# The low part of every weight split, subtracted on VectorE in place of GpSimd

## The chip, the cores and the metric

The kernel runs on one core of a Trainium2 chip. Its engines are TensorE (PE in the profile; PEld is its weight load), VectorE (DVE), ScalarE (ACT), GpSimd (POOL) and SyncE (SP, which issues the DMAs here). Each engine runs its own list of instructions in order and waits for the others through semaphores. The metric is the time on the device in microseconds (us), lower is better.

## The reference

One inference step of a two-layer decoder for 1024 new tokens of one sequence, 8 x 8 tokens of eight running sequences and 16 meta tokens, 1104 columns in all, model width 1024, everything in fp32:

```python
# layer 0
h = h + mamba_mixer(h, ...)        # RMSNorm, in_proj 1024 -> 6176, conv, SSD scan, gated norm, out_proj 2048 -> 1024
h = sq_relu_mlp(h, ...)            # h + square(relu(rmsnorm(h) @ w_up)) @ w_down, 1024 -> 4096 -> 1024
# between
k, v = shared_kv(h, ...)           # one K/V projection
# layer 1
h = h + swa(queries(h), k, v) @ w_o   # sliding window of 128, sinks
h = sq_relu_mlp(h, ...)
y = rmsnorm(h, ...)                # and the conv, SSM and K/V states
```

Nearly all of the arithmetic is in the products with the weights `w_in`, `w_out`, `w_up`, `w_down`, `w_kv`, `w_q`, `w_o`.

## The kernel before

**Split products.** TensorE takes operands rounded to fp32r. To keep fp32 precision each operand is written as a high part, rounded to fp32r, and a low part, the rest. `mm3` (L204 to L206) makes a product from three matmuls: high x high, high x low, low x high. So every weight has to be cast (high) and subtracted (low) on the chip before TensorE can use it; activations are split in the same way elsewhere (for instance at L1230 and L1146 for the inputs of the down product, L1012 for the up product).

**The two weight helpers.** `wunit` loads 128 x 1024 fp32 of a weight into a `raw` tile (two buffers), multiplies it by a norm weight on GpSimd for some (L168), casts it on ScalarE (L170), and subtracts (L171). With `keep` it writes both parts to DRAM, from where they come back later without a split. `wparts` does the same for a quarter block that is already in SBUF, 128 x 512 in the up product and 128 x 384 in the down and out products: cast on ScalarE (L1047), subtract (L1048). The results of both helpers lie in tiles `w`, of which there are six (for four of the units of the out projection's last block there are four more). A cast has to wait until TensorE has released a tile.

**Products of blocks.** The up products (`up_pair`), most of the down products and most of the out projection (`block_products`) compute a 2 x 2 block product with seven products in place of eight. `up_weights` and `down_weights` are generators that yield the seven weights of one output tile: four blocks as they are and three sums, which VectorE makes (L1057 and L1063, L1166 and L1172). The sum `s1` is changed in place at L1063 and L1172 after it was split, so that this step has to follow the subtraction at L1048. One product is 24 or 18 matmuls on two column halves into one of four PSUM tiles (`ma`, `mb`, `mc`, `md`, two banks each), which several of the seven products accumulate in turn. VectorE or ScalarE reads a PSUM tile after a product (L1077 in the up product, L1264 in the down product) before TensorE may go on in it. In the down product the seven inputs of the next block are loaded and split (L1230) while the last products of the block before and the first of the new one run: `make` gives the steps. L1146 splits the inputs of the plain block at the end.

**Stages, in order of time.** The mixer with convolution and SSD scan (to about 600 us), the gates with the grouped norm (to about 870; L763 to L817, with the sum of squares split at L248 and reduced on TensorE at L259 and L262), the out projection (to about 1030), the up product of layer 0 (to about 1460), its down product (to about 1750), K/V and attention (to about 2200), and the up and down products of layer 1 with the final norm. Weights of the attention are split ahead by `split_ahead` in earlier stages.

**What sets the order.** The instructions of an engine are not run in the order of the source: a planner simulates the kernel with its own estimates of every instruction's cost, and each engine gets its list in the order in which that simulation issues them. On the chip the list is fixed. Products and tile counts come from the source.

Of the kernel before, what the change touches and what calls it, by code (L numbers as in the profile page):

```python
# [8 lines left out]
F32 = mybir.dt.float32  # L9
F32R = mybir.dt.float32r  # L10
AF = mybir.ActivationFunctionType
ALU = mybir.AluOpType
# [129 lines left out]
class Kernel:  # L142
# [13 lines left out]
    def wunit(self, view, a, b, pre=None, to=None, key=None, keep=False):  # L156


        nc = self.nc
        if key in self.split:  # L160
            ws = [self.wtile([P, a, b]) for _ in range(2)]
            for e, w in enumerate(ws):
                nc.sync.dma_start(out=w.bitcast(F32), in_=self.split[key][:, e].rearrange("p (a b) -> p a b", b=b))
            return ws
        raw = self.raw([P, a, b])
        nc.sync.dma_start(out=raw, in_=view)
        if pre is not None:
            nc.gpsimd.tensor_tensor(out=raw, in0=raw, in1=pre, op=ALU.mult)  # L168
        wh, wl = ((to or self.wtile)([P, a, b]) for _ in range(2))
        nc.scalar.copy(out=wh, in_=raw)  # L170
        nc.gpsimd.tensor_tensor(out=wl, in0=raw, in1=wh.bitcast(F32), op=ALU.subtract)  # L171
        if keep:
            d = self.split[key] = self.dram.tile([P, 2, 1024], F32, name="ws_%s" % "_".join(map(str, key)))
            for e, w in enumerate((wh, wl)):
                nc.sync.dma_start(out=d[:, e].rearrange("p (a b) -> p a b", b=b), in_=w.bitcast(F32))
        return wh, wl
# [867 lines left out]
    def wparts(self, src, shape):  # L1044
        nc = self.nc
        t = self.wtile([P, 2] + shape)
        nc.scalar.copy(out=t[:, 0], in_=src)  # L1047
        nc.gpsimd.tensor_tensor(out=t[:, 1], in0=src, in1=t[:, 0].bitcast(F32), op=ALU.subtract)  # L1048
        return t[:, 0], t[:, 1]

    def up_weights(self, layer, f):
# [975 lines left out]
```

## Time and profile before

| | |
|---|---|
| three runs | 2921.8, 2928.17, 2928.39 us; median 2928.17 |
| span of the profiled execution | 2921.9 us, beside a lowest run of 2921.8 |
| mean granted clock of TensorE in it | 0.986 |
| GpSimd, the two subtractions (L171, L1048) | 96 and 476 instructions |
| GpSimd idle until ScalarE's casts ended (L170, L1047) | 189.3 and 609.6 us |
| bytes moved | 433 MB, 148 GB/s read and written over the span |

How to read it: a row of a group gives the line, the engine, the operation, output <- inputs, the shapes, the count, then busy us and mean ns of one, then the idle time of the engine before these instructions and what ended it. A row of the waits gives the engine and the line that waited, whom it waited for, and us in total, times, and the longest. Idle time of an engine that nothing waits for costs nothing, and a busy TensorE is not a TensorE at its peak, as the ends of its pipelined matmuls are modelled.

### The profile page before, as it was taken

To read this page: it belongs to the slowest core of one execution; us is meant where nothing else is said; L and a number is where in the kernel's file an instruction comes from. 1 tells how busy PE (TensorE), PEld (TensorE's weight loads), DVE (VectorE), ACT (ScalarE), POOL (GpSimd) and SP (SyncE) were. 2 spreads that over 40 slices of the span, in tenths; PEclk is the share of its full clock that TensorE was granted. 3 is DMA by queue.
4 is the path that set the end of the run, shared out by engine and by line. 5 is a ranking of instruction groups with operands and counts; after the bars stand their busy time and mean duration, and the time that the engine had idled before them with its cause. 6 is when DMAs were issued, how large, how long until landed. Compare 5 with 4: busy or idle time off the path is not lost.

```text
span 2921.9 us, 51729 instructions
## 1 busy us (share of the span) xinstructions
PE 2816.2 (96%) x19895; PEld 2711.0 (93%) x19895; DVE 1895.0 (65%) x2995; ACT 1413.9 (48%) x2742; POOL 1386.1 (47%) x1279
## 2 busy tenths in 40 slices
PE   8999999988989999999999999999999999999998
PEld 6999999978889999999999999988889999999998
DVE  6788777765657675455466765666678454356675
ACT  6555555544555264444343325655555444433333
POOL 5566666665546615444266573312112444345562
PEclk9999999999999999999999999999999999999998
DMA  3344544447655224444554422447453444533422
GB/s 137 91 128 124 125 128 123 123 123 258 218 206 171 80 85 149 136 156 139 224 212 171 161 89 94 160 153 261 164 187 133 150 140 150 206 138 124 151 96 73
DMA packets 219470, 433.43 MB, mean 148 GB/s; under 512 B 30728, under 2 KB 128392, under 8 KB 216648
## 3 DMA queue, kind: packets, MB, share of 16 engines
q1 hardware_dynamic: 219224, 430.14, 44.3%
q8 instruction: 156, 2.56, 0.4%
q14 instruction: 90, 0.74, 0.1%
HBM read 302.71 MB, written 128.32 MB: 148 GB/s over the span
## 4 chain that ended last, share of the span: by engine, by line
PE 77%; DVE 10%; ACT 4%; issue 3%; DMA 3%; POOL 3%; SPq 0%; DVEq 0%; ACTq 0%; POOLq 0%
PE g L204 10%; PE g L206 10%; PE g L205 10%; PE mc L204 4%; PE mc L206 3%; PE mc L205 3%; PE ma L204 3%; PE ma L205 3%; PE ma L206 3%; PE md L206 3%; PE md L205 3%; PE md L204 3%; PE mb L206 3%; PE mb L204 3%; PE mb L205 3%
## 5 line engine op out<-in xcount | busy, mean ns | idle before, releaser
L1048 POOL TENSOR_TENSOR w<-s,w 128x384 fp32r<-128x384 f32 (+1 forms) x272 | 370.4, 1368 | 386.9 <-ACT w L1047 354.4
L206 PE MATMUL g<-S,w 128*128 128x384 f32 (+2 forms) x1584 | 531.1, 336 | 3.9 <-POOL w L171 3.3
L204 PE MATMUL g<-S,w 128*128 128x384 f32 (+2 forms) x1584 | 533.4, 337 | 1.3 <-DVE qp L1462 0.6
L205 PE MATMUL g<-S,w 128*128 128x384 f32 (+2 forms) x1584 | 533.6, 337 | 0.0
L1048 POOL TENSOR_TENSOR w<-raw,w 128x384 fp32r<-128x384 f32 (+1 forms) x204 | 264.3, 1301 | 286.2 <-ACT w L1047 255.2
L171 POOL TENSOR_TENSOR w<-raw,w 128x1024 fp32r<-128x1024 f32 x96 | 247.1, 2574 | 253.3 <-ACT w L170 189.3
L206 PEld LDWEIGHTS g<-S,w 128*128 128x128 f32 x1584 | 301.9, 191 | 5.8 <-POOL w L171 3.6
L204 PEld LDWEIGHTS g<-S,w 128*128 128x128 f32 x1584 | 301.3, 190 | 4.7 <-issue 1.5
L205 PEld LDWEIGHTS g<-S,w 128*128 128x128 f32 x1584 | 301.7, 190 | 0.9 <-issue 0.3
L1047 ACT CAST w<-s 128x384 fp32r<-128x384 f32 (+1 forms) x272 | 149.8, 557 | 313.0 <-DVE s L1172 84.7
L204 PE MATMUL ma<-S,w 128*128 128x276 f32 (+1 forms) x808 | 235.2, 291 | 8.0 <-DVE us L1264 6.7
L206 PE MATMUL ma<-S,w 128*128 128x276 f32 (+1 forms) x808 | 234.7, 290 | 0.0
L205 PE MATMUL ma<-S,w 128*128 128x276 f32 (+1 forms) x808 | 234.3, 290 | 0.0
L1047 ACT CAST w<-raw 128x384 fp32r<-128x384 f32 (+1 forms) x204 | 111.8, 555 | 154.6 <-PE mc L206 45.2
L602 DVE SCALAR_TENSOR_TENSOR fm<-xp,cv,fm 128x1024 f32<-128x1024 f32 x96 | 162.8, 1698 | 33.1 <-ACT fm L583 32.5
L204 PEld LDWEIGHTS ma<-S,w 128*128 128x128 f32 x808 | 153.3, 190 | 9.3 <-ACT S L1229 2.7
L205 PE MATMUL g<-R,w 128*128 128x384 f32 (+2 forms) x480 | 158.6, 330 | 0.0
L204 PE MATMUL g<-R,w 128*128 128x384 f32 (+2 forms) x480 | 158.1, 329 | 0.0
L206 PE MATMUL g<-R,w 128*128 128x384 f32 (+2 forms) x480 | 158.1, 329 | 0.0
L205 PEld LDWEIGHTS ma<-S,w 128*128 128x128 f32 x808 | 153.5, 190 | 0.0
L206 PEld LDWEIGHTS ma<-S,w 128*128 128x128 f32 x808 | 153.2, 190 | 0.0
L170 ACT CAST w<-raw 128x1024 fp32r<-128x1024 f32 x96 | 100.5, 1047 | 105.8 <-DMA raw<-in_w_o_dram 19.9
(492 smaller groups left out, 8696.0 us busy)
## 6 DMA issues: line engine op xcount, KB each, us to landing
raw<-in_w_up_dram SPq DMA_DIRECT2D x64, 512.0 KB
raw<-in_w_in_dram SPq DMA_DIRECT2D x48, 512.0 KB
raw<-in_w_downs_dram SPq DMA_DIRECT2D x64, 384.0 KB
w<-ws_o SPq DMA_DIRECT2D x48, 512.0 KB
w<-ws_q SPq DMA_DIRECT2D x40, 512.0 KB
ab<-acs_d SPq DMA_DIRECT2D x64, 256.0 KB
S<-t_d SPq DMA_DIRECT2D x18, 828.0 KB
S<-t_e SPq DMA_DIRECT2D x18, 816.0 KB
```

The source lines that it names most:

```text
L170: nc.scalar.copy(out=wh, in_=raw)
L171: nc.gpsimd.tensor_tensor(out=wl, in0=raw, in1=wh.bitcast(F32), op=ALU.subtract)
L204: mm(out=out, lhsT=wh, rhs=xh, start=(first and k == 0), stop=False)
L205: mm(out=out, lhsT=wh, rhs=xl, start=False, stop=False)
L206: mm(out=out, lhsT=wl, rhs=xh, start=False, stop=(k == n - 1))
L602: nc.vector.scalar_tensor_tensor(out=acc[:, :SEQ], in0=xp[:, k:k + SEQ], scalar=cv[:, j, k:k + 1], in1=acc[:, :SEQ], op0=ALU.mult, op1=ALU ...
L1047: nc.scalar.copy(out=t[:, 0], in_=src)
L1048: nc.gpsimd.tensor_tensor(out=t[:, 1], in0=src, in1=t[:, 0].bitcast(F32), op=ALU.subtract)
```

## The change

The engine of the subtraction is another in both helpers. Nothing else in the source is changed: the operands, the tiles and their counts stay.

```diff
@@ wunit
         nc.scalar.copy(out=wh, in_=raw)
-        nc.gpsimd.tensor_tensor(out=wl, in0=raw, in1=wh.bitcast(F32), op=ALU.subtract)
+        nc.vector.tensor_tensor(out=wl, in0=raw, in1=wh.bitcast(F32), op=ALU.subtract)
@@ wparts
         nc.scalar.copy(out=t[:, 0], in_=src)
-        nc.gpsimd.tensor_tensor(out=t[:, 1], in0=src, in1=t[:, 0].bitcast(F32), op=ALU.subtract)
+        nc.vector.tensor_tensor(out=t[:, 1], in0=src, in1=t[:, 0].bitcast(F32), op=ALU.subtract)
```

On GpSimd remain the products and copies of the SSD scan and the convolution, the gate's product (L770), the multiplication by a norm weight (L168), some splits of activations and a few sums (L1288).

## The prediction

> **What bounds the kernel now.** I read the first part of the page (busy shares), then the waits of the matmul engine, then windows stage by stage, and inside the worst windows the groups by shape.
>
> ```profile
> span 2921.9 us, 51729 instructions
> PE 2816.2 (96%) x19895; PEld 2711.0 (93%) x19895; DVE 1895.0 (65%) x2995; ACT 1413.9 (48%) x2742; POOL 1386.1 (47%) x1279
> PE ms L262 <- DVE msl L248: 15.0, 5, 5.3
> PE md L204 <- ACT w L1047: 9.4, 2, 6.2
> PE mb L204 <- DVE hh L1264: 7.4, 2, 4.8
> PE ma L204 <- DVE us L1264: 6.7, 4, 2.5
> PE mc L204 <- DVE hh L1264: 3.7, 6, 1.0
> PE ma L204 <- DVE hh L1264: 3.4, 3, 1.2
> PE g L206 <- POOL w L171: 3.3, 1, 3.3
> PE md L206 <- POOL w L1048: 2.0, 2, 1.8
> ```
>
> PE is busy 2816 of 2922 us, so everything that can be won lies in 106 us of idle PE. The waits (total, times, longest) say who is to blame: VectorE's PSUM evacuations at L1264 with 7.4 + 6.7 + 3.7 + 3.4 = 21.2 us, VectorE's low part of the gate norm (L248) with 15.0, ScalarE's weight cast with 9.4, and the two subtractions that are moved with only 3.3 + 2.0 us. So GpSimd is rarely what PE waits for, and VectorE often is. By stage:
>
> ```profile
> 1168.00:1440.00 272.00, 272.00 (x2092) 272.00 (x2091) 136.36 (x172) 130.18 (x205) 113.06 (x83) 1.00 0.50 174
> 146.00:584.00 438.00, 435.73 (x2991) 400.07 (x2990) 350.14 (x604) 243.01 (x575) 289.88 (x362) 1.00 0.47 125
> 1513.00:1548.00 35.00, 31.59 (x235) 31.18 (x234) 27.30 (x25) 15.90 (x19) 21.47 (x13) 0.95 0.56 209
> 1548.00:1580.00 32.00, 32.00 (x254) 32.00 (x254) 19.02 (x24) 9.27 (x17) 19.89 (x16) 1.00 0.41 143
> 868.00:893.00 25.00, 19.84 (x129) 19.11 (x130) 24.11 (x22) 14.94 (x21) 18.19 (x11) 0.80 0.40 144
> ```
>
> After the length come PE, PEld, DVE, ACT, POOL busy, then PE's granted clock. In the up stage (first row) PE has no gap, with VectorE at half load; in the SSD stage (second) PE is idle 2.3 us of 438, VectorE at 80%. PE loses time where VectorE is full: at the change from one block of the down product to the next (third row, 3.4 us lost, VectorE 27.3 of 35; the quiet stretch after it loses nothing with VectorE at 19 of 32), and at the start of the out projection (last row, 5.2 us lost, VectorE 24.1 of 25).
>
> **The change part by part.** What leaves GpSimd, by shape, and the nearest VectorE rows for the same work:
>
> ```profile
> L171 POOL TENSOR_TENSOR w<-raw,w 128x1024 fp32r<-128x1024 f32 x96 | 247.1, 2574 | 253.3 <-ACT w L170 189.3 <-PE mc L206 22.5 <-PE mb L206 9.2
> L1048 POOL TENSOR_TENSOR w<-s,w 128x384 fp32r<-128x384 f32 x160 | 216.0, 1356 | 200.4 <-ACT w L1047 194.2 <-DMA raw<-in_w_outs_dram 2.2 <-DMA S<-t_e 1.9
> L1048 POOL TENSOR_TENSOR w<-s,w 128x512 fp32r<-128x512 f32 x112 | 154.4, 1384 | 186.4 <-ACT w L1047 160.2 <-DMA raw<-in_w_up_dram 25.4 <-DVE s L1063 0.8
> L1048 POOL TENSOR_TENSOR w<-raw,w 128x384 fp32r<-128x384 f32 x120 | 149.6, 1255 | 83.2 <-ACT w L1047 83.2
> L1048 POOL TENSOR_TENSOR w<-raw,w 128x512 fp32r<-128x512 f32 x84 | 114.7, 1367 | 203.0 <-ACT w L1047 172.0 <-DVE rx L1077 28.3 <-DVE s L1057 2.7
> L1669 DVE TENSOR_TENSOR S<-X,S x8: 546/549/553, 2178.0 to 2197.3; 128x384 fp32r<-128x384 f32 x8
> L1057 DVE TENSOR_TENSOR s<-raw,s 128x512 f32<-128x512 f32 x11 | 7.5, 679 | 0.0
> L1012 DVE TENSOR_TENSOR T<-t,T 128x1088 fp32r<-128x1088 f32 x4 | 5.1, 1280 | 0.0
> ```
>
> (The row of L1669 has shortest, median and longest in ns.) Removed from GpSimd: 247.1 + 216.0 + 154.4 + 149.6 + 114.7 = 881.8 us, so it falls from 1386 to about 504. Added to VectorE: 280 x 0.549 (the same operation and shape, fp32r out, both inputs in SBUF) = 154; 196 x 0.679 = 133; the 96 wide ones lie between 384 columns (549) and 1088 (1280), a slope of 1.04 ns a column, so 549 + 640 x 1.04 = 1.21 us each, 117. Together 404 us, an estimate from those rows. VectorE would stand at 1895 + 404 = 2299 us, 79%, if nothing got cheaper.
>
> Something does get cheaper. VectorE's operations with two SBUF inputs run longer while GpSimd works:
>
> ```profile
> L1166 DVE TENSOR_TENSOR s<-raw 128x384 f32<-128x384 f32 x80 | 81.6, 1059 | 5.6 <-DMA raw<-in_w_downs_dram 5.6
> L171 POOL TENSOR_TENSOR w<-raw,w x96: 2343/2398/8552, 10.5 to 2866.4; 128x1024 fp32r<-128x1024 f32 x96
> ```
>
> The weight sums at L1166 average 1059 ns where 549 is the free price. The second row gives minimum, median and maximum of one GpSimd operation of one shape: 2.34, 2.40 and 8.55 us, so GpSimd can be held up by some 6 us as well. The Trainium skill, in "SBUF — State Buffer", section "Who interferes with whom", says that GpSimd shares a port pair with VectorE and that whichever starts first holds it for its whole instruction; the 8.55 agrees that one can be shut out, while 1059 beside 549 is a mean over collisions and can't show a whole instruction's block. The prices below are these rows' own.
>
> The place that decides is the block change in the down product, where VectorE has no gap. All of its work, and GpSimd's, from 1518 to 1544 us:
>
> ```profile
> L1230 DVE TENSOR_TENSOR S<-S 128x1656 fp32r<-128x1656 f32 x5 | 10.5, 2111 | 3.6 <-ACT S L1229 3.6
> L1230 DVE TENSOR_TENSOR A<-A 128x1656 fp32r<-128x1656 f32 x2 | 4.4, 2220 | 0.0
> L1172 DVE TENSOR_TENSOR s<-s,raw 128x384 f32<-128x384 f32 x2 | 1.9, 947 | 0.3 <-POOL w L1048 0.3
> L1166 DVE TENSOR_TENSOR s<-raw 128x384 f32<-128x384 f32 x2 | 1.8, 960 | 0.0
> L1166 DVE TENSOR_TENSOR s<-raw,s 128x384 f32<-128x384 f32 x2 | 1.4, 719 | 0.0
> 1518.77 1.88 DVE L1230 TENSOR_TENSOR S<-S 128x1656 fp32r<-128x1656 f32 x1 [3.58 <-ACT S L1229]
> L1048 POOL TENSOR_TENSOR w<-s,w 128x384 fp32r<-128x384 f32 x7 | 13.5, 1940 | 10.8 <-ACT w L1047 10.8
> L1048 POOL TENSOR_TENSOR w<-raw,w 128x384 fp32r<-128x384 f32 x3 | 5.3, 1751 | 0.5 <-ACT w L1047 0.5
> ```
>
> Ten subtractions come over: 10 x 0.549 = 5.5 us. Relief: the seven splits of L1230 took 14.9 us, at the undisturbed 1.88 they take 13.2, so 1.7; the six sums at L1166 and L1172 took 5.1 us, at 0.549 they take 3.3, so 1.8; the 0.3 us that L1172 waited for GpSimd before overwriting its operand goes, since both are now on one engine. Net 5.5 - 3.8 = +1.7 us of VectorE work in a stretch with no free time. What is late next is the evacuation at L1264 that frees the PSUM bank, and PE stands for it. There are three such changes in each layer's down product. In layer 1 VectorE is less full:
>
> ```profile
> 2628.00:2663.00 35.00, 34.06 (x270) 33.65 (x268) 24.99 (x25) 18.69 (x24) 20.21 (x15) 1.00 0.59 213
> ```
>
> PE loses 0.9 us there, with VectorE at 25 of 35, so part of the new work finds room; I take 1.0 for these. 3 x 1.7 + 3 x 1.0 = **+8.1 us**. Bounds: -12 (2 us regained in each, if operations pack more tightly than their durations) to +33 (no relief: 5.5 each).
>
> Other terms:
> - *Direct waits for GpSimd.* The 3.3 us are the 8.55 us operation that was shut out; at 1.21 us it goes. The 2.0 us shrink with 1.3 becoming 0.55: take 1.2. **-4.5** (0 to -5.3).
> - *Starts of the product stages.* The 9.4 us for the cast at L1047 are 6.2 + 3.2 at two such starts. At the first the chain that ended last holds a moved operation:
>
> ```profile
> 871.30 2.51 POOL w L1048
> ```
>
>   2.51 us becomes 0.55 plus VectorE's queue, which is full there (24.1 of 25). I take **-3** for both (0 to -9.4).
> - *Gates (657 to 876 us).* The first row below counts the wide operations there; the other two show a collision in the chain to L248, for which PE waits 15.0 us:
>
> ```profile
> L171 POOL TENSOR_TENSOR w<-raw,w 128x1024 fp32r<-128x1024 f32 x18 | 46.1, 2559 | 18.9 <-DMA ws_q<-w 7.8 <-ACT w L170 7.4 <-DMA ws_kv<-w 3.6
> L817 DVE TENSOR_TENSOR gm<-gy,gm 128x552 f32<-128x552 f32 x6 | 12.9, 2148 | 0.0
> L1264 DVE TENSOR_TENSOR us<-ma,us 128x552 f32<-128x552 f32 x16 | 11.6, 723 | 7.9 <-PE ma L206 7.9
> ```
>
>   18 x 1.21 = 22 us come to VectorE and 46 leave GpSimd. L817 takes 2148 ns beside 723 for the same width. GpSimd's gate product stays and collides too, so I take **-3** (-8 to +5).
> - *SSD stage (146 to 584 us).*
>
> ```profile
> L171 POOL TENSOR_TENSOR w<-raw,w 128x1024 fp32r<-128x1024 f32 x24 | 61.1, 2546 | 27.8 <-ACT w L170 27.8
> ```
>
>   24 x 1.21 = 29 us come to 350 of 438, 87% with no relief. PE idles 2.3 us now; I take **0** because the 88 us that VectorE now has idle hide it (-2 to +15 if they don't).
> - *Up stages.* PE has no gap, VectorE goes from 136 to at most 192 of 272 (GpSimd's 113 us there are some 82 operations of 1.38, at 0.679 on VectorE 56 us). **0.** That a blocked VectorE doesn't reach PE here is in the trace:
>
> ```profile
> DVE s L1057 <- DMA raw<-in_w_up_dram: 84.2, 24, 6.5
> ```
>
>   It stands 84 us for weight loads, up to 6.5 at once, mostly in these stages, and PE doesn't notice.
>
> The change adds no DMA and no instruction, and moves nothing past SP's or POOL's DMA issue; a subtraction that ends sooner lets the spill of a split weight start sooner, which is costed at nothing. It does add one kind of wait to VectorE's queue: the subtraction waits for ScalarE's cast, and behind it stand the evacuations that PE waits for (rival 2).
>
> Sum: 8.1 - 4.5 - 3 - 3 = -2.4 us on the profiled execution, 2921.9 to 2919.5. That span equals the lowest of the three runs (2921.8), so nothing measurable lies around it; two of three runs lie at 2928, 6.3 us above, and so does the median. With that the forecast is 2919.5 + 6.3 = **2926 us**, no change (own range 2917 to 2935). 0.3%, 8.8 us, is about what a measurement of this kernel can tell from no change.
>
> **The rivals.**
> 1. *Faster: the collisions were the cost.* 882 us of GpSimd work is replaced by 404 of VectorE work, and if in the full stretches the pair of engines was really one resource, these stretches shorten. For it: 6 to 7 us of PE lost from 868 to 893, where the rows double. Against: PE is not idle elsewhere. Block changes +0, direct -5.3, starts -6, gates -8: -19 from the median's 2928, **2909 us**.
> 2. *Slower: the wait moves onto the engine that frees PSUM.* GpSimd could stand for ScalarE's cast (10.8 + 0.5 us in the 26 us above) at no cost. On VectorE the same stand holds the next L1264. Price: if a third of it, 3.8 us, falls on VectorE in each of the six changes, 23 us more: -2.4 + 23 = +21, with the clock's 0.95 in those stretches (23 / 0.95 = 24) +22, **2950 us**. It decides as soon as VectorE's list has a subtraction ahead of an evacuation whose product is finished; against it, the program's order is planned, and the splits at L1230, which wait for ScalarE in the same way, stood only 3.6 us here, before the full stretch. The Trainium skill, "Perfetto Trace Analysis", section "Optimizing Scalar/DVE Operations", says that where VectorE is saturated, handing work to GpSimd may make sense, but may not help as the two share a port; that speaks against taking it back here. The trace shows saturation only in those stretches.
> 3. *It does more than it says.* The order on every engine is planned anew with other costs; in the SSD stage (VectorE 80%) a worse order would show first: +15, **2943 us**.
>
> **How the numbers follow.** Forecast 0.40, rival 1 0.30, rival 2 0.25, rival 3 0.05. Faster by over 0.3%: 0.30. Within: 0.40. Slower: 0.30. The range reaches below rival 1 to all gains together, 2900, and above rival 2 to the block changes with no relief and part of the stand, 2960.
>
> **What would show it.** Right: the 384-wide subtraction near 0.55 us on VectorE, VectorE near 2150 to 2250 busy, GpSimd near 500, L1166 near 0.55 to 0.7, no PE wait for POOL, L1264 waits of 20 to 32 us. Rival 1: L1264 and L248 waits clearly under 36 together. Rival 2: VectorE rows "w <- ACT w L1047" with tens of us, inside the block changes, and PE waits on L1264 of 40 or more. Wrong altogether: gaps of PE in the SSD or the up stages.

## The result and the profile after

| | before | after |
|---|---|---|
| median (runs) | 2927.69 us (4) | 2906.31 us (4) |
| lowest to highest | 2921.8 to 2928.39 | 2904.78 to 2909.76 |
| span of the profiled execution | 2921.9 | 2905.5 |

The ratio is 0.9933, with a 95% interval of 0.9919 to 0.9947: the kernel is faster by 0.67%, some 20 us. The forecast was no change (2926); the time and the direction of rival 1 (2909) are what came. On the profiled spans the gain is 16.4 us: TensorE's idle time fell by 12.9 us (2921.9 - 2816.2 = 105.7 before, 2905.5 - 2812.7 = 92.8 after), and its busy time by 3.5.

The first part of the page after, its span and its busy shares:

```profile
span 2905.5 us, 51403 instructions
...
PE 2812.7 (97%) x19895; PEld 2707.2 (93%) x19895; DVE 2065.7 (71%) x3567; ACT 1418.8 (49%) x2742; POOL 513.2 (18%) x707
```

GpSimd fell from 1386 to 513 us, as the subtractions' rows said. VectorE rose by only 171 us. The groups of VectorE by shape (busy us, mean ns of one, then idle time before them) show both halves of that:

```profile
L171 DVE TENSOR_TENSOR w<-raw,w 128x1024 fp32r<-128x1024 f32 x96 | 124.1, 1293 | 48.5 <-ACT w L170 36.4 <-issue 4.7 <-PE ma L206 3.2
L1048 DVE TENSOR_TENSOR w<-s,w 128x384 fp32r<-128x384 f32 x160 | 90.3, 570 | 13.9 <-ACT w L1047 13.9
L1048 DVE TENSOR_TENSOR w<-s,w 128x512 fp32r<-128x512 f32 x112 | 76.8, 687 | 54.7 <-ACT w L1047 54.6
L1048 DVE TENSOR_TENSOR w<-raw,w 128x384 fp32r<-128x384 f32 x120 | 65.8, 558 | 2.0 <-ACT w L1047 1.8
L1048 DVE TENSOR_TENSOR w<-raw,w 128x512 fp32r<-128x512 f32 x84 | 57.9, 691 | 14.5 <-ACT w L1047 14.1
...
L1166 DVE TENSOR_TENSOR s<-raw 128x384 f32<-128x384 f32 x80 | 44.6, 594 | 4.0 <-DMA raw<-in_w_downs_dram 3.5 <-DMA raw<-in_w_outs_dram 0.5
```

The subtractions take 124.1 + 290.8 = 414.9 us on VectorE. So its other work became 1895.0 + 414.9 - 2065.7 = 244 us cheaper, with the same instructions: L1166 fell from 1059 to 594 ns, beside 549 undisturbed. 882 us of GpSimd work thus turned into a net 171 us of VectorE work.

What TensorE waits for after the change (us in total, times, longest):

```profile
PE ms L259 <- ACT gm L795: 10.3, 6, 3.5
...
PE mb L206 <- DVE w L1048: 5.9, 2, 2.9
PE ma L204 <- DVE us L1264: 5.9, 5, 2.2
PE md L204 <- ACT w L1047: 5.4, 2, 3.2
...
PE mb L204 <- DVE us L1264: 3.4, 4, 1.4
...
PE ms L262 <- DVE msl L248: 3.2, 3, 1.5
```

The waits for L1264 fell from 21.2 us to 11.4 (all rows of that line), those for L248 from 15.0 to 3.2. No row names GpSimd any more. Two waits grew: that for L795, the gates' next link, from 1.1 to 10.3 us, and those for the moved subtractions themselves, from 5.5 us on GpSimd (3.3 + 2.0 + 0.2) to 9.0 on VectorE (5.9 + 2.2 + 0.9).

**Where the 16.4 us lie.** The rows of the evacuations at L1264, asked for in each block stage, mark its start (first `hh<-md`) and end (last `hh<-mb`); the rows below some of them say who waited. Before, the out projection, then the down products of layers 0 and 1:

```profile
L1264 DVE TENSOR_TENSOR hh<-md,hh x8: 717/726/733, 880.8 to 989.8; 128x552 f32<-128x552 f32 x8
...
L1264 DVE TENSOR_TENSOR hh<-mb,hh x8: 717/726/733, 899.0 to 1005.8; 128x552 f32<-128x552 f32 x8
...
L1264 DVE TENSOR_TENSOR hh<-md,hh x16: 716/720/733, 1467.7 to 1721.7; 128x552 f32<-128x552 f32 x16
...
L1264 DVE TENSOR_TENSOR hh<-mb,hh x16: 716/722/734, 1480.1 to 1736.6; 128x552 f32<-128x552 f32 x16
...
  PE ma L204: 8.3, 5
  PE mb L204: 4.8, 1
...
L1264 DVE TENSOR_TENSOR hh<-md,hh x16: 706/721/726, 2596.1 to 2837.7; 128x544 f32<-128x544 f32 x16
...
L1264 DVE TENSOR_TENSOR hh<-mb,hh x16: 707/724/727, 2609.9 to 2853.6; 128x544 f32<-128x544 f32 x16
```

And after:

```profile
L1264 DVE TENSOR_TENSOR hh<-md,hh x8: 718/724/734, 875.4 to 987.3; 128x552 f32<-128x552 f32 x8
...
L1264 DVE TENSOR_TENSOR hh<-mb,hh x8: 715/724/733, 893.8 to 1003.3; 128x552 f32<-128x552 f32 x8
...
L1264 DVE TENSOR_TENSOR hh<-md,hh x16: 715/723/733, 1455.2 to 1702.5; 128x552 f32<-128x552 f32 x16
...
L1264 DVE TENSOR_TENSOR hh<-mb,hh x16: 718/726/734, 1468.6 to 1715.6; 128x552 f32<-128x552 f32 x16
...
  PE mb L204: 4.5, 4
  PE ma L204: 1.7, 3
...
L1264 DVE TENSOR_TENSOR hh<-md,hh x16: 708/720/726, 2576.6 to 2821.6; 128x544 f32<-128x544 f32 x16
...
L1264 DVE TENSOR_TENSOR hh<-mb,hh x16: 708/725/726, 2590.1 to 2837.5; 128x544 f32<-128x544 f32 x16
```

| stretch | before | after | change |
|---|---|---|---|
| to the start of the out projection | 880.8 | 875.4 | -5.4 |
| out projection, block products | 125.0 | 127.9 | +2.9 |
| its last units and the up product of layer 0 | 461.9 | 451.9 | -10.0 |
| down product of layer 0 | 268.9 | 260.4 | -8.5 |
| K/V, attention, up product of layer 1 | 859.5 | 861.0 | +1.5 |
| down product of layer 1 | 257.5 | 260.9 | +3.4 |
| to the end | 68.3 | 68.0 | -0.3 |

So there are three gains and two losses, and the largest gain lies in a place for which the prediction shows no window.

**That place, 1000 to 1120 us.** The window before, then after (length, then PE, PEld, DVE, ACT, POOL busy, then PE's clock):

```profile
1000.00:1120.00 120.00, 114.51 (x684) 113.91 (x684) 79.89 (x120) 62.52 (x97) 38.47 (x16) 0.97 0.32 101
```

```profile
1000.00:1120.00 120.00, 120.00 (x757) 120.00 (x756) 93.46 (x146) 69.89 (x108) 0.00 (x0) 1.00 0.37 122
```

TensorE lost 5.5 us, 3.3 for a wide subtraction and 2.2 for a step of the norm (L247), and its granted clock was 0.97; after, it is full at 1.00. The lower clock follows the gaps: cut into slices of 10 us, the stretch before has a clock of 0.83 from 1050 to 1060, where the gap of 2.2 us lies, and from 1100 to 1110, right behind the one of 3.3, and 1.00 in all the others. So a gap cost more than its own length. Over the whole stretch of the table TensorE was busy for 456.4 of 461.9 us before and for all of the 451.9 after: of the 10.0 us, 5.5 were idle and 4.5 are busy time. VectorE was only two thirds busy, which is why I passed this stretch over. The timeline before (start, length, idle time before it) shows what happened, on GpSimd, on VectorE and on SyncE's queue:

```profile
1090.75 8.55 POOL L171 TENSOR_TENSOR w<-raw,w 128x1024 fp32r<-128x1024 f32 x1 [39.81 <-ACT w L170]
...
1089.71 1.30 DVE L1012 TENSOR_TENSOR T<-hh,T 128x1104 fp32r<-128x1104 f32 x1
1090.93 1.30 DVE L989 TENSOR_TENSOR hh<-hh 128x1104 f32<-128x1104 f32 x1
...
1094.59 2.52 DVE L1012 TENSOR_TENSOR T<-hh,T 128x1104 fp32r<-128x1104 f32 x2
1103.40 1.29 DVE L1057 TENSOR_TENSOR s<-raw 128x512 f32<-128x512 f32 x2 [6.30 <-DMA raw<-in_w_up_dram]
...
1099.33 0.33 SPq L1041 DMA_DIRECT2D raw<-in_w_up_dram  x1
```

VectorE ran L1012 and L989 in turn, without a pause, until 1094.59 + 2.52 = 1097.11: each operation starts 0.08 us before the one ahead of it ends. When GpSimd's subtraction began at 1090.75, the L1012 of 1089.71 was still running. The subtraction ended at 1099.30, 2.2 us after VectorE had paused; undisturbed it takes 2.34 to 2.40. So while VectorE ran it made next to no progress, and TensorE waited for it (the 3.3 us row of the prediction). The Trainium skill, "SBUF — State Buffer", section "Who interferes with whom", says that the port pair which the two share is an exclusive lock, and that the order of issue decides who is blocked. The trace agrees, as VectorE's operation had started first, and shows one thing more: the block lasted over a row of six VectorE operations, five of which started after GpSimd's. The delay also ran on: the subtraction's `raw` tile came free at 1099.30, the next weight load was issued into it at 1099.33, and VectorE stood 6.30 us for that load. That part reached no wait of TensorE: its only two waits from 1000 to 1120 us are the two above. After the change:

```profile
1086.91 1.21 DVE L171 TENSOR_TENSOR w<-raw,w 128x1024 fp32r<-128x1024 f32 x1
...
1093.52 1.28 DVE L1057 TENSOR_TENSOR s<-raw 128x512 f32<-128x512 f32 x2
```

The wide subtraction takes 1.21 us, and L1057 starts without a wait. Over the whole run VectorE's standing for these loads (L1057) falls from 84.2 to 26.4 us.

**The first block change of layer 0's down product.** The stretch from the start of the first of seven splits at L1230 to the start of the last one, as a window; before:

```profile
1518.80:1541.10 22.30, 18.89 (x135) 18.48 (x134) 22.03 (x20) 13.33 (x16) 16.04 (x9) 0.92 0.59 225
```

after:

```profile
1506.40:1526.20 19.80, 18.38 (x139) 17.57 (x138) 19.79 (x24) 13.18 (x15) 0.00 (x0) 1.00 0.67 224
```

and some of VectorE's timeline in it, after:

```profile
1514.10 1.87 DVE L1230 TENSOR_TENSOR S<-S 128x1656 fp32r<-128x1656 f32 x1
...
1516.53 0.55 DVE L1048 TENSOR_TENSOR w<-s,w 128x384 fp32r<-128x384 f32 x1
1517.00 0.55 DVE L1048 TENSOR_TENSOR w<-raw,w 128x384 fp32r<-128x384 f32 x1
```

VectorE is full in both. It runs 24 operations in place of 20 (seven subtractions came, two evacuations and one sum run later now), and is through in 19.8 us in place of 22.3; TensorE loses 1.4 us in place of 3.4, and its granted clock is 1.00 in place of 0.92. The splits, 2.1 and 2.2 us on average before, last 1.87 again. Over the whole stage the 8.5 us are 4.7 of idle time of TensorE (13.4 before, 8.7 after) and 3.8 of busy time, at a clock of 1.00 in place of 0.97.

**Windows that answer to those of the prediction:**

```profile
146.00:584.00 438.00, 437.95 (x2995) 402.90 (x2994) 360.96 (x624) 241.44 (x569) 235.01 (x336) 1.00 0.47 126
868.00:893.00 25.00, 24.11 (x170) 23.60 (x171) 20.93 (x31) 15.63 (x23) 0.00 (x0) 0.89 0.40 145
1168.00:1440.00 272.00, 272.00 (x2067) 271.85 (x2066) 168.09 (x256) 127.22 (x196) 0.00 (x0) 1.00 0.48 169
...
2610.00:2645.00 35.00, 32.99 (x263) 32.80 (x262) 26.04 (x36) 18.02 (x23) 0.00 (x0) 1.00 0.62 213
```

The SSD and the up stage are full, as predicted. In layer 1's first block change TensorE now loses 2.0 us where it lost 0.9: there, VectorE's added work is not paid back.

**A new wait, for the subtraction itself.** Of TensorE's 9.0 us for moved subtractions, 5.9 are two single waits of 2.9 us, one in the block change of the out projection, until 943.7 us, and one in a block change of layer 1's down product, until 2779.1. The second, asked for in that stage (2570 to 2840 us), and VectorE's own wait for the casts over the whole run:

```profile
PE mb L206 <- DVE w L1048: 2.9, 1, 2.9
...
DVE w L1048 <- ACT w L1047: 84.4, 61, 2.8
```

In neither place did VectorE stand for the cast: that had ended 5.6 and 6.3 us before the subtraction started, and VectorE worked without a pause in between, on the evacuations, splits and sums that stand ahead of the subtraction in its list. On GpSimd the subtraction had a list of its own; on VectorE it is late itself where VectorE is full. Each of the two stages that became longer, by 2.9 and 3.4 us, holds one such wait of 2.9; neither had one before.

### The profile page after: what moved, and what is told of

Read it like the earlier page. It is cut to its first block, busy times and chain, and to the rows that moved or that the text cites. A ratio compares the mean times of both kernels' runs of the same rounds, so it can differ in the third digit from the quotient of the medians.

```text
span 2905.5 us, 51403 instructions
## 1 busy us (share of the span) xinstructions
PE 2812.7 (97%) x19895; PEld 2707.2 (93%) x19895; DVE 2065.7 (71%) x3567; ACT 1418.8 (49%) x2742; POOL 513.2 (18%) x707
## 4 chain that ended last, share of the span: by engine, by line
PE 82%; DVE 8%; DMA 4%; ACT 3%; issue 2%; POOL 1%; SPq 0%; DVEq 0%; POOLq 0%; ACTq 0%
PE g L204 11%; PE g L205 11%; PE g L206 11%; PE mc L204 4%; PE mc L206 4%; PE mc L205 4%; PE ma L204 4%; PE ma L206 4%; PE ma L205 4%; PE md L206 3%; PE md L205 3%; PE md L204 3%; PE mb L204 3%; PE mb L206 3%; PE mb L205 3%
## 5 line engine op out<-in xcount | busy, mean ns | idle before, releaser
L1288 POOL TENSOR_TENSOR hh<-hh,us 128x552 f32<-128x552 f32 (+1 forms) x24 | 36.3, 1534 | 1501.5 <-DVE us L1264 1501.5
L1048 DVE TENSOR_TENSOR w<-s,w 128x384 fp32r<-128x384 f32 (+1 forms) x272 | 167.0, 618 | 68.5 <-ACT w L1047 68.5
L171 DVE TENSOR_TENSOR w<-raw,w 128x1024 fp32r<-128x1024 f32 x96 | 124.1, 1293 | 48.5 <-ACT w L170 36.4
L204 PE MATMUL mc<-S,w 128*128 128x276 f32 (+1 forms) x512 | 148.2, 289 | 0.2 <-DVE hh L1264 0.2
```

The source lines that it names most:

```text
L171: nc.vector.tensor_tensor(out=wl, in0=raw, in1=wh.bitcast(F32), op=ALU.subtract)
L204: mm(out=out, lhsT=wh, rhs=xh, start=(first and k == 0), stop=False)
L1048: nc.vector.tensor_tensor(out=t[:, 1], in0=src, in1=t[:, 0].bitcast(F32), op=ALU.subtract)
L1288: e.tensor_tensor(out=to, in0=to, in1=uv, op=ALU.add)
```

## The experiments

Two theories stood against each other. **A**: VectorE and GpSimd took turns at reading SBUF, and the gain is the collisions that are gone, less the price of VectorE's added work. **B**: the instructions are the same, but with other costs the planner writes other lists, and these happened to be better. All times are compared with the kernel before on the same chip, where it had medians of 2924.08 (e1 to e4), 2923.72 (e5 to e8) and 2924.70 us (e9, e10).

**One helper at a time.** Two kernels, each with one of the two lines of the diff:

```diff
@@ e1: before, wunit only
-        nc.gpsimd.tensor_tensor(out=wl, in0=raw, in1=wh.bitcast(F32), op=ALU.subtract)
+        nc.vector.tensor_tensor(out=wl, in0=raw, in1=wh.bitcast(F32), op=ALU.subtract)
@@ e2: before, wparts only
-        nc.gpsimd.tensor_tensor(out=t[:, 1], in0=src, in1=t[:, 0].bitcast(F32), op=ALU.subtract)
+        nc.vector.tensor_tensor(out=t[:, 1], in0=src, in1=t[:, 0].bitcast(F32), op=ALU.subtract)
```

> Only the 96 wide subtractions (L171) run on VectorE; the 476 of L1048 stay on GpSimd. Theory A (the two engines had been taking turns at reading SBUF, and the gain is the collisions that went): the gain at the way from the out projection to the first up stage (1030 to 1120 us, where PE went from 114.5 to 120 busy of 120) comes back, 6 to 11 us; nothing in the down stages, whose collisions are with L1048. Time 2917 to 2922. Theory B (the gain is a luckier order from the planner): a third order, so anything from 2905 to 2935, and the stretch from 1030 to 1120 not regained in particular.

> Only the 476 subtractions of L1048 run on VectorE; the 96 wide ones stay on GpSimd. Theory A: the down stage of layer 0 regains its 6 to 9 us, the start of the out projection some 5, the way to the first up stage loses PE time as before. Time 2912 to 2919, and the gains of this run and of e1_wunit add up to the whole (about 21 us). Theory B: no sum is to be expected.

e1: 2916.48 us, 0.9975 (0.9965 to 0.9986). e2: 2913.51 us, 0.9961 (0.9947 to 0.9975). The two gains, 0.25% and 0.39%, add up to 0.64%; together they brought 0.67%. They lie in different stages (table below): e1 lets the out projection start 3.2 us sooner, shortens the stretch behind it by 8.2 us and leaves the down product of layer 0 as it was; e2 shortens that down product by 11.8 us. One piece of A's expectation failed: e2 does not bring the start of the out projection forward (881.6 us, 880.8 before); that gain is the wide subtractions'. Lists that happened to be better would hardly split by the place of the moved operations like this.

**GpSimd's reads put back.** The kernel after, with reads of GpSimd of 128 columns each behind every L1048, into a tile that is used for nothing: one read for each 128 columns in e3 (1624 in all), two for each subtraction in e5 (`range(2)`, 952).

```diff
@@ wparts
         nc.vector.tensor_tensor(out=t[:, 1], in0=src, in1=t[:, 0].bitcast(F32), op=ALU.subtract)
+        for q in range(shape[0]):
+            nc.gpsimd.tensor_tensor(out=self.dummy, in0=t[:, 0, q].bitcast(F32), in1=self.dummy, op=ALU.subtract)
```

> The changed kernel, and behind each subtraction of L1048 GpSimd reads the same high part in 3 or 4 pieces of 128 columns and writes a scratch tile that nobody uses: GpSimd is as busy as before (some 500 to 700 us more), and no one waits for it. Theory A: the weight sums at L1166 go from 0.59 back to 0.9 to 1.1 us, L1230 from 1.88 to 2.0 or more, VectorE's busy time rises by 80 us or more, each block change loses 2 to 5 us more, time 2915 to 2945. Theory B: within 4 us of the changed kernel, 2902 to 2910.

> As e3_reads, but GpSimd reads only two pieces of 128 columns behind each subtraction of L1048, so that its extra work is near the 635 us that the change took from it at this line (e3_reads put in some 1100 and cost 53 us over the changed kernel). Theory A: 20 to 35 us over the changed kernel, that is 2924 to 2940 beside 2924 for the kernel before, and stalls at the block changes of the size of e3_reads' in proportion. If nothing but e3_reads' overdose cost time: under 8 us over the changed kernel.

e3: 2959.02 us, 1.0115 (1.0100 to 1.0130). e5: 2941.72 us, 1.0057 (1.0038 to 1.0075). Against 0.9933 that is +1.82% (53 us) and +1.24% (36 us), for 1094 and 697 us of GpSimd's reads. From the page of e5, its row of the weight sums (L1173 is L1166 there), and its rows in layer 0's down product (L1271 is L1264):

```profile
PE 2820.5 (96%) x19895; PEld 2713.2 (92%) x19895; DVE 2175.4 (74%) x3572; ACT 1416.6 (48%) x2742; POOL 1210.8 (41%) x1659
...
L1173 DVE TENSOR_TENSOR s<-raw 128x384 f32<-128x384 f32 x80 | 58.5, 767 | 3.1 <-DMA raw<-in_w_downs_dram 3.1
```

```profile
L1271 DVE TENSOR_TENSOR hh<-md,hh x16: 717/720/722, 1464.0 to 1728.2; 128x552 f32<-128x552 f32 x16
...
L1271 DVE TENSOR_TENSOR hh<-mb,hh x16: 719/720/734, 1476.2 to 1739.1; 128x552 f32<-128x552 f32 x16
...
  PE ma L204: 6.3, 4
```

Both times lie above what A was expected to give (2945 and 2940 at most), while the weight sums rise less than expected: from 594 ns to 767 in e5 and 784 in e3, not to 900 or more. VectorE does the same work as after but for five small fills, and it takes 110 us more (2175.4 beside 2065.7). The down product takes 275.1 us in place of 260.4. The reads do hold the weight tiles, and ScalarE's cast stood 29.5 us for them in e5, but TensorE's waits for that cast rose only from 5.4 to 10.8 us, while its waits for the evacuations rose from 11.4 to 24.1. So A's mechanism has a large price here, most of it not by way of the casts.

**No subtraction at all, and a third of it.** e4 leaves out every subtraction of both helpers: GpSimd fills the low parts with a constant. e8 subtracts only the first 128 columns in `wparts` and GpSimd fills the rest.

```diff
@@ e4, both helpers
-        nc.vector.tensor_tensor(out=t[:, 1], in0=src, in1=t[:, 0].bitcast(F32), op=ALU.subtract)
+        nc.gpsimd.memset(t[:, 1].bitcast(F32), 1e-5)
@@ e8, wparts
-        nc.vector.tensor_tensor(out=t[:, 1], in0=src, in1=t[:, 0].bitcast(F32), op=ALU.subtract)
+        nc.vector.tensor_tensor(out=t[:, 1, 0:1], in0=src[:, 0:1], in1=t[:, 0, 0:1].bitcast(F32), op=ALU.subtract)
+        nc.gpsimd.memset(t[:, 1, 1:].bitcast(F32), 1e-5)
```

> Left out: all weight subtractions; GpSimd fills the low parts with a constant in their place, which reads no SBUF, so there is neither the work on VectorE nor a collision. Theory A with a price of the load on VectorE: block changes lose under 1.5 us each in place of about 3, time 2885 to 2898. If the load on VectorE costs nothing: 2903 to 2909, as the changed kernel. Theory B: not below 2900 for any reason of load.

> Left out: L1048 subtracts only the first 128 of its 384 or 512 columns on VectorE, GpSimd fills the rest with a constant (writes only). The number of instructions, the waits for the cast and the order of dependences stay, VectorE's work at this line falls from 291 to some 135 us. If the time that e4_no_sub won (44 us less than the changed kernel) is VectorE's load: about half of it, 2880 to 2890. If it is the wait for the cast in VectorE's list: 2898 to 2906.

e4: 2862.37 us, 0.9786 (0.9771 to 0.9801). e8: 2893.25 us, 0.9895 (0.9880 to 0.9910). The first part of e4's page:

```profile
PE 2795.5 (98%) x19895; PEld 2696.5 (94%) x19895; DVE 1699.5 (59%) x2995; ACT 1422.6 (50%) x2742; POOL 804.0 (28%) x1279
```

This splits the result. Beside a kernel without them, the low parts cost 2924 - 2862 = 62 us on GpSimd, and 0.9933 - 0.9786 = 1.47%, 43 us, on VectorE. The change swaps one price for the other, and both are large; the 20 us are their difference. Each price is that of the whole step: collisions or load, but also that a constant need not wait for the cast (TensorE's 9.0 us for the subtraction go too), and the constant changes what TensorE multiplies, which was not tried apart. e4 went below the range expected for A (2885 to 2898), so the step on VectorE costs more than I had thought. e8 shows the second price in part: 148 us less on VectorE (1918.0) are 11 us of time. That lies between the two ranges set for it, so it decides between load and wait only in part.

**The gates' product.** e6 is the kernel after with L770, GpSimd's product in the gates, on VectorE too.

```diff
@@ gates, L770
-                nc.gpsimd.tensor_tensor(out=yv[j], in0=g2[:, j], in1=yv[j], op=ALU.mult)
+                nc.vector.tensor_tensor(out=yv[j], in0=g2[:, j], in1=yv[j], op=ALU.mult)
```

> The changed kernel, and the gate's product (L770, 48 operations with two SBUF inputs, about 1.1 us each on GpSimd) on VectorE too. Theory A carried on: the last GpSimd work beside VectorE in the gates goes, the chain to the gate norm gets shorter, 3 to 8 us less than the changed kernel, 2896 to 2902. Against it: VectorE gets 48 x 0.55 = 26 us in a chain that it is part of; then 0 to 5 us more, 2904 to 2910.

2905.51 us, 0.9937 (0.9923 to 0.9951): no change against the kernel after, and a miss for A. The out projection starts 2.2 us sooner (873.2), and that is lost again before the end. TensorE's wait for L795 stays at 9.5 us, so the collision of L770 is not what makes it. It comes with the wide subtractions: it is there in e1 (8.0 us) and not in e2 or e10 (1.1). Why is open.

**Layer 1 left on GpSimd.** e7 is the kernel after with L1048 on GpSimd in the down product of layer 1, where the stage had become longer.

```diff
@@ wparts
-        nc.vector.tensor_tensor(out=t[:, 1], in0=src, in1=t[:, 0].bitcast(F32), op=ALU.subtract)
+        e = nc.gpsimd if self.late and shape[0] == KB else nc.vector
+        e.tensor_tensor(out=t[:, 1], in0=src, in1=t[:, 0].bitcast(F32), op=ALU.subtract)
```

> The changed kernel, but in the down product of layer 1 the subtraction stays on GpSimd. That stage ran 258.2 us before and 261.6 after, while layer 0's ran 269.6 and 261.1. Theory A with VectorE's load as the price at the block changes: layer 1's stage goes back to 258 to 259, 2 to 4 us less than the changed kernel, 2900 to 2903. If the difference of the two layers is chance of the order: 0 to 3 us more.

2906.42 us, 0.9939 (0.9926 to 0.9953). The whole time stays that of the kernel after, so the expected 2900 to 2903 was missed. The stage itself went from 260.9 to 258.3 us (before: 257.5), and TensorE's wait of 2.9 us for the subtraction is gone from it, so the loss there goes with the engine's choice; but 2.6 us are below what the whole time can tell.

**Only the eight wide ones behind the out projection.** e10 is the kernel before, with L171 on VectorE for the last four units of the out projection and four plain units of the first up product.

```diff
@@ wunit
-        nc.gpsimd.tensor_tensor(out=wl, in0=raw, in1=wh.bitcast(F32), op=ALU.subtract)
+        (lo or nc.gpsimd).tensor_tensor(out=wl, in0=raw, in1=wh.bitcast(F32), op=ALU.subtract)
@@ out_last
-            ws = [self.wunit(self.i["w_out4"][v], 4, 256, to=None if v < 2 else more) for v in range(4)]
+            ws = [self.wunit(self.i["w_out4"][v], 4, 256, to=None if v < 2 else more, lo=self.nc.vector) for v in range(4)]
@@ plain_up
-        ws = [self.wunit(self.i["w_up"][layer, f], KT, P, key=("up", f) if layer else None) for f in fs]
+        ws = [self.wunit(self.i["w_up"][layer, f], KT, P, key=("up", f) if layer else None, lo=None if layer else self.nc.vector) for f in fs]
```

> The kernel before, with the wide subtraction of wunit on VectorE only for the last units of the out projection (w_out4) and the plain units of the first up product (w_up of layer 0), which run between about 1000 and 1130 us; all the other wide ones and all of the 384- and 512-column ones stay on GpSimd. There the kernel before shows wide subtractions shut out for 6 to 8 us and TensorE 5.5 us short of full. If these few collisions are where the gain of moving the wide ones comes from: 4 to 7 us under the kernel before, a ratio of 0.9975 to 0.9985, and most of what moving all 96 brings (0.9975). If that gain is spread over all the wide ones, or comes from another planned order: within 2 us, a ratio of 0.9993 or more.

2920.09 us, 0.9983 (0.9974 to 0.9992). The row of the moved ones and the same window as above:

```profile
L171 DVE TENSOR_TENSOR w<-raw,w x8: 1215/1216/1669, 998.1 to 1091.1; 128x1024 fp32r<-128x1024 f32 x8
```

```profile
1000.00:1120.00 120.00, 118.98 (x740) 117.97 (x739) 86.14 (x132) 66.88 (x103) 23.25 (x11) 1.00 0.37 122
```

Eight of 572 subtractions bring 0.17%, of the 0.25% that all 96 wide ones bring, and the stretch behind the out projection shrinks from 461.9 to 454.3 us. A gain that is tied to eight operations, at the place where the trace shows one of them shut out, speaks for A. It also shows what the shut-out costs by itself: at the same place a subtraction of L1048 is now shut out on GpSimd, for 10.16 us from 1091.79, and TensorE loses only 1.0 of the 120 us. Here the price went by who waited, not by the length.

**A mixture.** e9 is the kernel after with L770 on VectorE as in e6, and L1048 back on GpSimd in the out projection and in layer 1's down product.

```diff
@@ wparts
-        nc.vector.tensor_tensor(out=t[:, 1], in0=src, in1=t[:, 0].bitcast(F32), op=ALU.subtract)
+        e = nc.gpsimd if self.lo_pool else nc.vector
+        e.tensor_tensor(out=t[:, 1], in0=src, in1=t[:, 0].bitcast(F32), op=ALU.subtract)
@@ block_products
+        self.lo_pool = nb == 2 or nn < T // 2
```

> The kernel after, with three pieces dealt out by the stage: the gate's product at L770 goes to VectorE as well (so that the gates have nothing of that size on GpSimd), and the subtraction of wparts goes back to GpSimd in two stages, the out projection's block products and the down product of layer 1, where the traces of the kernel after show the stage 2.7 and 3.4 us longer than before. Collisions as the cost, with each stage on its own: 2.7 + 3.4 = 6 us at most under the kernel after, 2900 to 2904 us, a ratio to the kernel before near 0.992. If a stage's loss is not the engine's choice there but what the planner makes of the whole list, or if the collisions return with the work: 2905 to 2912, a ratio of 0.9935 or more, and the out projection still about 129 us.

2903.24 us, 0.9921 (0.9907 to 0.9934). The interval overlaps that of the kernel after, so it can't be told apart from it. The two stages do shorten by 1.1 and 2.9 us, and neither has a wait of TensorE of 2.9 us for the subtraction any more; the down product of layer 0, whose code is as after, became 2.6 us longer.

The stages of all of these, from the same rows (us; the waits are TensorE's for L1264, summed over the run):

| kernel | start of out proj. | out proj. | to down 0 | down 0 | to down 1 | down 1 | waits |
|---|---|---|---|---|---|---|---|
| before | 880.8 | 125.0 | 461.9 | 268.9 | 859.5 | 257.5 | 21.2 |
| after | 875.4 | 127.9 | 451.9 | 260.4 | 861.0 | 260.9 | 11.4 |
| e1 wide only | 877.6 | 126.0 | 453.7 | 269.6 | 866.1 | 257.7 | 17.4 |
| e2 narrow only | 881.6 | 127.5 | 459.2 | 257.1 | 860.5 | 259.3 | 9.2 |
| e3 reads | 876.8 | 132.9 | 455.7 | 283.7 | 859.3 | 276.7 | 32.9 |
| e4 none | 860.2 | 123.0 | 451.6 | 253.5 | 856.7 | 248.4 | 1.4 |
| e5 fewer reads | 879.6 | 131.1 | 453.3 | 275.1 | 862.2 | 269.8 | 24.1 |
| e6 gate | 873.2 | 128.6 | 454.3 | 258.5 | 860.6 | 259.6 | 13.0 |
| e7 layer 1 | 876.4 | 126.9 | 452.9 | 260.5 | 861.0 | 258.3 | 13.9 |
| e8 a third | 874.2 | 126.5 | 453.6 | 257.2 | 861.2 | 251.3 | 3.5 |
| e9 mixture | 870.3 | 126.8 | 452.5 | 263.0 | 863.4 | 258.0 | 16.3 |
| e10 eight | 881.7 | 125.0 | 454.3 | 270.7 | 862.2 | 257.6 | 17.9 |

B is not needed for any of the large differences; it isn't excluded as a part of them, as every kernel here has lists of its own. B, or the spread from one execution to the next, can explain the scatter: the stages are read from one profiled execution each, and stages whose code is the same differ by 2 to 5 us from kernel to kernel (down 0 in after, e6, e7 and e9: 258.5 to 263.0). Single stage differences of that size, the attention's +1.5 among them, stay open where no wait shows them. So does e1's +6.6 us between the down products, whose profiled execution (2920.73 us) ran 4 us above the median of its kernel.

## Where the prediction was right and where it was wrong

The median of 2906 us lies inside the wide range of 2900 to 2960, at the end of it that was drawn for rival 1, but below the forecast's own 2917 to 2935, and the kernel got faster where no change was forecast. Sum of the forecast: -2.4 us on the profiled span; measured: -16.4. By its steps:

- **"Everything that can be won lies in 106 us of idle PE": not quite.** Idle time gave 12.9 of the 16.4 us. In the two stretches that gained most, 4.5 and 3.8 us were busy time, at a clock that no longer fell with the gaps; elsewhere busy time rose by 4.8. The forecast had no term for it.
- **Block changes, +8.1: wrong in sign in layer 0, the step that failed most.** Measured -8.5 in layer 0's down product and +3.4 in layer 1's, together -5.1. The mechanism (VectorE is full there, collisions stretch its work, the evacuation is late) was right: the waits for L1264 fell by half. Its size was not. I set ten subtractions at 0.549 us against 3.8 us of relief, +1.7. In the stretch of the first change that I compared there are seven, and they start 0.47 us apart (1516.53 and 1517.00): 3.3 us in place of 5.5. The relief was near the forecast: 22.3 + 3.3, less 1.75 for the three operations that left (by spacings of 0.64, 0.64 and 0.47 us), less 19.8, is 4.0. So the net is -0.7 there where I had +1.7, and VectorE's full stretch gets shorter, not longer; the other 1.75 of its 2.5 us are operations that run later now, which is order and not work. My lower bound, "if operations pack more tightly than their durations", named one of the reasons and was not taken. The other two changes of layer 0 were not taken apart, and the rest of the 8.5 us includes the 3.8 of busy time above. For layer 1 the term of 3 x 1.0 met the size (+3.4) by luck: the stage holds the wait of 2.9 us for the subtraction itself, which I had not priced.
- **Direct waits for GpSimd, -4.5: wrong.** The wait of 3.3 us for the shut-out operation went, as forecast, and its stretch gained 10.0: with the other wait there and the clock, three times what I had priced. But TensorE's waits for the moved subtractions did not fall from 5.5 us, they rose to 9.0: I took an operation of 0.55 us in place of 1.3 to be awaited for less time, and left out that it now queues behind VectorE's other work. I had the row of 84.2 us of VectorE's standing for the weight loads in a fence and read it as harmless ("PE doesn't notice"); two thirds of it went, and no wait of TensorE shows that this gained time.
- **Starts -3 and gates -3:** measured -5.4 up to the start of the out projection and +2.9 in it. At the start I priced a subtraction of L1048; e1 and e2 show that the gain came with the wide ones. In the gates the collision that I named went (L817 from 2148 to 724 ns), and the wait for L248 fell by 11.8 us, but 9.2 us came back one link further, at L795 (1.1 us before, 10.3 after). So the size was met by a compensation that I had not named; e6 shows that L770's collisions are not behind it.
- **SSD 0, up stages 0: right.** TensorE is full in both windows; VectorE's 29 us there cost it only 11 (350.14 to 360.96).
- **The 6.3 us on top** were too much. I set the span of the profiled execution beside the time of another one: in all later executions the time stands 1.7 to 2.9 us above the execution's own span (2907.35 beside 2905.5 after the change), and the kernel before had medians of 2924 in the later comparisons.
- **Rival 1** had the cause and nearly the time (2909), but with terms that came out otherwise: block changes 0 (measured -5.1), direct waits -5.3 (they rose by 3.5, while the stretch of the longest gained 10.0), gates and starts -14 (-2.5). The 6 to 7 us of lost PE that it quotes for 868 to 893 are 5.2 in its own row.
- **Rival 2:** its wait exists. VectorE stands 84.4 us for casts at L1048 and 36.4 at L171, but TensorE's waits for L1264 fell, and in the block change of layer 0 that was taken apart no subtraction waited. Its price, 23 us, was not paid. What came instead is the reverse, 5.9 us: not the evacuation behind the subtraction was late, but the subtraction behind the evacuations and splits.
- **Rival 3** did not come in the SSD stage, where it was to show.

"No change" rested on relief and load nearly cancelling. They do largely cancel, 62 against 43 us by e4, but I had both too small, and counted relief only as shorter durations of operations on VectorE, without the lower clock that comes with TensorE's gaps.

## What to carry to other kernels

Where two engines take turns at a memory, price a move between them as one resource: what the pair does after the move against what it did, not the durations of one engine alone. Look for the longest single duration of a fixed shape (8.55 us beside 2.40), and ask who waits for its end: the one of 8.55 us held TensorE, the one of 10.16 us in e10 hardly did. Ask of the moved operation too where it will stand in the list of its new engine, and who waits for it there. A stage where the engine is far from full can hold the larger gain.

## What the runs showed that I had not expected

- A GpSimd operation was shut out not for one VectorE operation but for a whole row of them, for as long as they followed on each other: 8.55 us, of which the last 2.2 are about its whole undisturbed time.
- TensorE's granted clock was 0.83 in the two slices of 10 us with or right behind its gaps of 2.2 and 3.3 us, and 1.00 in the ten others from 1000 to 1120 us. After the change, without the gaps, it was 1.00 throughout.
- VectorE's operations start closer together than they last, so that sums of durations overstate a full stretch: the subtractions of 128x384 last 0.55 us and start 0.47 apart, 15% less, the splits last 1.87 and the next operation starts 1.79 behind them, 4% less.
- GpSimd's reads cost where TensorE's next step hangs on VectorE and almost nothing elsewhere: in e5 the three block stages became 3.2, 14.7 and 8.9 us longer than after, the stretches with the up products 1.4 and 1.2.
